# Low-part products last, ranks in two pieces, and a deeper split-ahead in a one-core decoder step

## The chip, the core and the metric

The kernel runs on one core of one Trainium2 chip. The metric is the device time of one execution in microseconds (us); several executions are made and their median is quoted. PE is the matrix engine (PEld its weight loads), DVE, ACT and POOL are the vector, scalar and GpSimd engines, SP issues most of the transfers.

## The reference

One layer of a decoder: 512 prompt tokens and 32 sample tokens of width 1024, through a mixer (projection, pooling, a stabilised mLSTM, an output projection) and then product-key retrieval over 16384 single-neuron experts:

```python
q = (xb @ w_q).reshape(blk, PEER_HEADS, 2, HALF_KEY)
s = jnp.einsum('nhpc,hpkc->nhpk', q, keys)
sv, si = lax.top_k(s, TOPK)                       # 16 of 128 keys, for each half
comb = sv[:, :, 0, :, None] + sv[:, :, 1, None, :]
top, sel = lax.top_k(comb, TOPK)                  # 16 of 256 pairs
eidx = ...                                        # the experts that the pairs name
g = jax.nn.softmax(top, axis=-1)
act = jax.nn.gelu(jnp.einsum('nd,nhkd->nhk', xb, u_tab[eidx]))
y = jnp.einsum('nhk,nhkd->nd', g * act, v_tab[eidx])
```

## The kernel before

**Products in two parts.** Every large float32 product is made of three matmuls: each operand is split into a high and a low part, and hi x hi, hi x lo and lo x hi are summed in PSUM (the accumulator banks). For weights ACT makes the high part `whi` (a rounding copy, line 443) and DVE or POOL the low part `wlo` = raw - whi (line 445). A weight block goes through three places: a load into one of four `raw` buffers (SP, line 418), the split into one of four `whi`/`wlo` pairs, and the products. The class `Weights` walks a list of blocks: `deep` is how many split blocks it holds ahead of the one in use, `early` how many loaded ones beyond that. The list also says which engine makes the low part.

**Where the three products stand.** `part` (called by `proj`, for the first projections and for the queries `half_q`), `out_mm` (the output projection), `uphase` (the experts' first table) and `ymm` (the second table) each issue hi·hi, hi·lo, lo·hi for every chunk before they go to the next one, so the low part of the weights is wanted by the third matmul.

**The retrieval.** 384 of the 512 prompt tokens are done densely: `uphase(b)` multiplies them by a block of 128 experts of `u_tab` (24 matmuls of 384 columns into `pH`, then a Gelu on ACT); there are 128 blocks, U0 to U127 below. `ymm` multiplies the gated activations by the block of `v_tab` (18 matmuls of 512 columns into six banks `Y`). The other 128 prompt tokens and the sample tokens gather their experts' rows one by one (POOL issues the gathers, DVE does the arithmetic).

**The order around the change.** The queries run in two halves (`halves`); four U blocks (`PRE`) are put among the second. DVE sorts the scores (`top16`, `best`). Then comes one loop, which mixes U blocks on PE with a generator `topks` on DVE: `ranks` (indices of the pairs), `topk` for five groups of tokens, transposes on PE (`gates_in`) and 48 groups of gate products (`gates_of`: one-hot tiles `E` and `P` on DVE, 16 matmuls each into `pg` on PE, a copy to `stage` on ACT, a write to DRAM `Gd`). Which comes next in the program is decided by a small model in that loop: `pe` and `dve` are its clocks, `PEU`, `PEG`, `LOU`, `GRP` its prices, `TOFF` DVE's lead time at the start, and each `yield` of `topks` a price in us. `lo_at` holds when low parts are ready. The loop may run blocks only up to `AHEAD - RES`; the rest up to `AHEAD` follow it and cover the time until the first gates are back from DRAM.

After the loop SP is given five loads of spilled activations (`ar`), the first load of gates (`load_g`, tile `gr`), more U blocks and the first blocks of `v_tab` (tile `vr`, which shares the four `raw` buffers). Activations of U blocks below `SPILL = AHEAD - RING` went to DRAM. In the last stage each V block (`vprep`, then `ymm`) is done alone until 13 activations are left on the chip, and from there with one U block each; `pace` spreads 320 gather steps over it.

The engines work their instructions in the order of the program, each its own; SP's transfers too are issued in order.

## Time and profile before

| | |
|---|---|
| three timed runs | 1651.47, 1658.17, 1670.41 us (median 1658.17) |
| the profiled execution | 1654.74 us, span 1653.0 us |
| PE busy / DVE busy / ACT busy / POOL busy | 94% / 82% / 38% / 42% of the span |
| mean granted clock of PE | 0.972 of full speed |
| transfers | 454.16 MB, mean 275 GB/s |

A timeline row gives the start, the duration, the engine, the source line, the operation, out<-in with shapes, how many, and in brackets how long the engine had been idle before and what ended that. A row of stretches gives start:end, length, and busy time of PE, PEld, DVE, ACT and POOL with their instructions, then the granted clock of PE (1.00 is 2.4 GHz; 0.5 would be 1.2 GHz all through), the busy share of the transfer engines and GB/s.

### The profile page before, as it was taken

Reading aid. Unit: us, or ns where it says so; the run is one execution under the profiler, and the core shown is the slowest. Engines: PE = TensorE matmul, PEld = TensorE weight load, DVE = VectorE, ACT = ScalarE, POOL = GpSimd, SP = SyncE. Lnnn points to the kernel's source line nnn. Section 1 sums busy time; section 2 is a strip of 40 time slices with the busy share of each in tenths; the row PEclk is TensorE's granted clock in tenths of the full one; section 3 lists DMA queues with packets and bytes.
Section 4 is the critical chain, followed back from the end, with each engine's and each line's share of the span. In section 5 each row is a group of like instructions: output and inputs, shape, how many; then the busy total and the mean of one; then the engine's idle time right before and its main releaser. Section 6 shows DMA issues by size and latency. Waiting matters only on the chain.

```text
span 1653.0 us, 25192 instructions
## 1 busy us (share of the span) xinstructions
PE 1560.3 (94%) x9293; PEld 1385.3 (84%) x9293; DVE 1349.8 (82%) x2738; ACT 630.5 (38%) x999; POOL 702.0 (42%) x517
## 2 busy tenths in 40 slices
PE   5999999897998999999999999999999999999994
PEld 3888777586998989998778899999999999999873
DVE  6644467698999899985888888988888898988986
ACT  4322223545533345553333333333333333333343
POOL 2343333456551000004233356656566666566615
PEclk9999988998999999999999999999999999999997
DMA  8544446554343558869999999999999999999981
GB/s 343 178 144 160 144 147 173 191 182 128 114 142 118 170 175 289 302 245 378 379 356 382 344 336 368 370 365 359 370 376 358 359 371 363 366 370 359 368 282 67
DMA packets 180272, 454.16 MB, mean 275 GB/s; under 512 B 23152, under 2 KB 83440, under 8 KB 178484
## 3 DMA queue, kind: packets, MB, share of 16 engines
q1 hardware_dynamic: 119448, 246.31, 43.5%
q0 software_dynamic: 46080, 167.79, 27.0%
q10 hardware_dynamic: 14620, 38.44, 6.2%
q8 instruction: 73, 1.20, 0.3%
q14 instruction: 51, 0.42, 0.1%
HBM read 412.34 MB, written 40.14 MB: 274 GB/s over the span
## 4 chain that ended last, share of the span: by engine, by line
PE 74%; DVE 13%; DMA 5%; issue 3%; ACT 2%; POOL 2%; SPq 0%; ACTq 0%; POOLq 0%; DVEq 0%
PE Y L160 27%; PE pH L160 27%; PE bk L160 10%; PE tb L160 4%; PE pg L160 3%; DMA gr<-Gd 2%; PE pm L160 1%; DVE wlo L445 1%; DMA wm<-in_w_mod_r_dram 1%; POOL wlo L445 1%; DMA raw<-in_u_b_dram 1%; PE tb L164 1%; DVE i L1108 1%; DVE scr L1106 1%; DVE scr L1111 1%
## 5 line engine op out<-in xcount | busy, mean ns | idle before, releaser
L1433 POOL DMA_INDIRECT rbuf<-in_u_tab_dram,eid x160 | 211.9, 1324 | 421.8 <-DMA ar<-Ad 235.3
L160 PE MATMUL pH<-u2hi,wlo 128*128 128x384 f32 x992 | 334.8, 338 | 6.9 <-DVE wlo L445 6.8
L160 PE MATMUL pH<-u2hi,whi 128*128 128x384 f32 x992 | 339.8, 343 | 0.4 <-ACT act L1192 0.4
L160 PE MATMUL pH<-u2lo,whi 128*128 128x384 f32 x992 | 335.1, 338 | 0.0
L1433 POOL DMA_INDIRECT rbuf<-in_v_tab_dram,eid x160 | 244.5, 1528 | 188.7 <-DVE y L1458 133.2
L160 PE MATMUL Y<-whi,chi 128*128 128x512 f32 x768 | 300.5, 391 | 5.3 <-ACT chi L1499 5.3
L160 PE MATMUL Y<-whi,clo 128*128 128x512 f32 x768 | 301.9, 393 | 3.5 <-DVE clo L1500 2.3
L160 PE MATMUL Y<-wlo,chi 128*128 128x512 f32 x768 | 301.3, 392 | 0.0
L443 ACT ACTIVATE whi<-raw 128x1024 fp32r<-128x1024 f32 (+1 forms) x193 | 203.0, 1055 | 218.7 <-issue 174.3
L443 ACT ACTIVATE whi<-vr 128x1024 fp32r<-128x1024 f32 x128 | 135.6, 1060 | 283.3 <-PE Y L160 243.2
L445 DVE TENSOR_TENSOR wlo<-vr,whi 128x1024 fp32r<-128x1024 f32 x128 | 156.7, 1224 | 91.7 <-ACT whi L443 87.9
L445 POOL TENSOR_TENSOR wlo<-raw,whi 128x1024 fp32r<-128x1024 f32 (+2 forms) x64 | 149.7, 2348 | 156.7 <-ACT whi L443 155.3
L1458 DVE SCALAR_TENSOR_TENSOR y<-rbuf,cf,y 128x1024 f32<-128x1024 f32 x158 | 202.5, 1282 | 0.9
L160 PEld LDWEIGHTS pH<-u2hi,wlo 128*128 128x128 f32 x992 | 186.9, 188 | 8.9 <-DVE wlo L445 8.9
L445 DVE TENSOR_TENSOR wlo<-raw,whi 128x1024 fp32r<-128x1024 f32 (+1 forms) x133 | 161.9, 1220 | 37.4 <-ACT whi L443 37.2
L160 PEld LDWEIGHTS pH<-u2hi,whi 128*128 128x128 f32 x992 | 187.2, 189 | 3.8 <-ACT act L1192 0.7
L160 PEld LDWEIGHTS pH<-u2lo,whi 128*128 128x128 f32 x992 | 187.1, 189 | 2.9
L160 PEld LDWEIGHTS Y<-whi,chi 128*128 128x128 f32 x768 | 144.8, 189 | 37.5 <-ACT chi L1499 7.3
L160 PEld LDWEIGHTS Y<-whi,clo 128*128 128x128 f32 x768 | 144.8, 188 | 34.3 <-DVE clo L1500 4.1
L160 PEld LDWEIGHTS Y<-wlo,chi 128*128 128x128 f32 x768 | 144.7, 188 | 30.1
L1446 DVE SCALAR_TENSOR_TENSOR rbuf<-rbuf,utok 128x1024 f32<-128x1024 f32 x128 | 156.1, 1222 | 0.0
L1192 ACT ACTIVATE act<-pH 128x384 f32<-128x384 f32 x124 | 59.4, 479 | 111.1 <-PE pH L160 111.1
(402 smaller groups left out, 2583.1 us busy)
## 6 DMA issues: line engine op xcount, KB each, us to landing
raw<-in_u_b_dram SPq DMA_DIRECT2D x128, 512.0 KB
vr<-in_v_tab_dram SPq DMA_DIRECT2D x128, 512.0 KB
wm<-in_w_mod_r_dram SPq DMA_DIRECT2D x48, 512.0 KB
gr<-Gd SPq DMA_DIRECT2D x32, 768.0 KB
Gd<-stage ACTq DMA_DIRECT2D x9, 2048.0 KB
raw<-in_w_q_b_dram SPq DMA_DIRECT2D x32, 512.0 KB
raw<-in_w_in_b_dram SPq DMA_DIRECT2D x20, 512.0 KB
Ad<-act ACTq DMA_DIRECT2D x40, 192.0 KB
```

The source lines that it names most:

```text
L160: nc.tensor.matmul(out, l, r, start=start, stop=stop, skip_group_check=True)
L164: nc.tensor.transpose(out, x, idn)
L443: nc.scalar.activation(hi, raw, AF.Copy)
L445: e.tensor_tensor(lo[:, d], raw[:, d], f32(hi[:, d]), op=ALU.subtract)
L1106: nc.vector.max(v[:, k], x)
L1108: nc.vector.max_index(i[:, k], v[:, k], x)
L1111: nc.vector.match_replace(x, v[:, k], x, -3.0e38)
L1192: nc.scalar.activation(x, p[:, 0:ND], AF.Gelu)
L1433: nc.gpsimd.indirect_dma_start(out=g, out_offset=None, in_=tab, in_offset=bass.IndirectOffsetOnAxis(ap=eid[t][:, k:k + 1], axis=0))
L1446: nc.vector.scalar_tensor_tensor(g, g, 1.0, u, op0=ALU.mult, op1=ALU.mult, accum_out=dots[:, k:k + 1])
L1458: nc.vector.scalar_tensor_tensor(y2[t], g, cf[:, k:k + 1], y2[t], op0=ALU.mult, op1=ALU.add)
```

## The change

Five things are changed.

1. In `part`, `out_mm`, `uphase` and `ymm` all products with the low part of the weights stand behind those with the high part: for a U block 16 matmuls with `whi`, then 8 with `wlo`; for `ymm` the two column halves alternate within each of the three products.
2. `ranks` becomes a generator with two prices (3.0 and 5.5) in place of one of 8.5, so U blocks' work may be put between its two pieces.
3. `WI.deep` is 3 in the loop (it was 2), and 2 again after it. The low part of one more U block is made on POOL (`PLO` = 4 in place of 3).
4. The loop's model: `TOFF` 14 in place of 10, low parts wanted `LOL` = 2.5 us after a block's start, `lo_at` with four places.
5. `AHEAD` 55 and `RES` 6 in place of 53 and 4. The loop may still run up to block 48; `SPILL` goes from 40 to 42.

```diff
-AHEAD = 53
+AHEAD = 55
-RES = 4
+RES = 6
+LOL = 2.50
+PLO = 4
-TOFF = 10.00
+TOFF = 14.00
...
     def part(p, w, m, i, dh, dl, cs=CORD):
         hi, lo = w[:2]
-        for c in cs:
-            for k, (x, u) in enumerate(((hi, dh), (hi, dl), (lo, dh))):
-                mm(p[:m, 0:WIDTH[i]], x[:, c, :], u[:, c, HALVES[i]],
-                   c == CORD[0] and k == 0, c == CORD[-1] and k == 2)
+        todo = [(c, x, u) for c in cs for x, u in ((hi, dh), (hi, dl))] + [(c, lo, dh) for c in cs]
+        for n, (c, x, u) in enumerate(todo):
+            mm(p[:m, 0:WIDTH[i]], x[:, c, :], u[:, c, HALVES[i]],
+               c == CORD[0] and n == 0, c == CORD[-1] and n == len(todo) - 1)
...
-    jobs += [(a["u_b"][b], 128, ON_POOL if b < ub + 3 else ON_DVE) for b in range(ub, NB)]
+    jobs += [(a["u_b"][b], 128, ON_POOL if b < ub + PLO else ON_DVE) for b in range(ub, NB)]
...
     def out_mm(p, t, c, w, n):
-        for i in range(2):
-            for k, (y, v) in enumerate(((yhi, hi), (ylo, hi), (yhi, lo))):
-                mm(p[i], y[:, c, cols_of[t]], v[:, 512 * i:512 * (i + 1)], n == 0 and k == 0, n == 7 and k == 2)
+        for ys in (((yhi, hi), (ylo, hi)), ((yhi, lo),)):
+            for i in range(2):
+                for y, v in ys:
+                    mm(p[i], y[:, c, cols_of[t]], v[:, 512 * i:512 * (i + 1)],
+                       n == 0 and y is yhi and v is hi, n == 7 and v is lo)
...
     def uphase(b, where=hbank):
-        for c in range(8):
-            for w, u in ((hi, u2hi), (hi, u2lo), (lo, u2hi)):
-                mm(p[:, 0:ND], w[:, c, :], u[:, c, DOFF:DOFF + ND], n == 0, n == 23)
-                n += 1
+        todo = [(c, hi, u) for c in range(8) for u in (u2hi, u2lo)] + [(c, lo, u2hi) for c in range(8)]
+        for n, (c, w, u) in enumerate(todo):
+            mm(p[:, 0:ND], w[:, c, :], u[:, c, DOFF:DOFF + ND], n == 0, n == 23)
...
         nc.vector.tensor_copy(cf_, ci)
+        yield 3.0
         ii = grl.tile([128, 16, HS], F16, name="ii")
...
         sx = grl.tile([128, HS], F32, name="sx2")
+        yield 5.5
         return ex, sx, ii, jj
...
-        r = ranks()
-        yield 8.5
+        r = yield from ranks()
...
+    WI.deep = 3
-    pe, dve, wait, freed, lo_at = 0.0, TOFF, [], [], [0.0, 0.0]
+    pe, dve, wait, freed, lo_at = 0.0, TOFF, [], [], [0.0] * PLO
...
-            pe = max(pe, lo_at.pop(0)) + PEU
-            dve = max(dve, pe - 2 * PEU) + LOU
-            lo_at.append(dve + 0.2)
+            pe = max(pe, lo_at.pop(0) - LOL) + PEU
+            if b + WI.deep > ub + PLO:
+                dve = max(dve, pe - PEU) + LOU
+                lo_at.append(dve + 0.2)
...
+    WI.deep = 2
...
     def ymm(b, t, parts=(slice(0, 512), slice(512, D))):
-        for d in parts:
-            y = Y[t][d.start // 512][:, d.start % 512:d.start % 512 + d.stop - d.start]
-            mm(y, ch[:, s], hi[:, d], b == 0, False)
-            mm(y, cl[:, s], hi[:, d], False, False)
-            mm(y, ch[:, s], lo[:, d], False, b == NB - 1)
+        for k, (c, v) in enumerate(((ch, hi), (cl, hi), (ch, lo))):
+            for d in parts:
+                y = Y[t][d.start // 512][:, d.start % 512:d.start % 512 + d.stop - d.start]
+                mm(y, c[:, s], v[:, d], b == 0 and k == 0, b == NB - 1 and k == 2)
```

What the loop's model makes of it, counted in PE's order of the two programs: before, 8 U blocks (U4 to U11) stand ahead of the first transposes, after, 11 (U4 to U14); 3, 4 and 4 blocks follow between the next transposes and the first gate products in both. The first gate products thus stand behind U22 before and behind U25 after. Then one U block and two groups of gate products alternate; in both programs six U blocks stand between the last gate products and the first V block, U47 to U52 before and U49 to U54 after, and after, the last three groups stand together with no U block among them. 40 V blocks are done alone before, 42 after.

On DVE, at the start of the loop, the low parts of U blocks (`wlo`) and `ranks` (`ex` to `jj`) stood before as

```order
L445 TENSOR_TENSOR wlo<-raw,whi 128x1024
L1239 TENSOR_TENSOR ex<-top 128x544
L1242 TENSOR_SCALAR rtmp<-sel 128x544
L1243 CAST rtmp<-rtmp 128x544
L1244 TENSOR_SCALAR rtmp<-sel 128x544
L1245 CAST rtmp<-rtmp 128x544
L1248 SCALAR_TENSOR_TENSOR rtmp<-rtmp 128x544
L1249 TENSOR_SCALAR rtmp<-rtmp 128x544
L1250 TENSOR_TENSOR ii<-rtmp 128x544
L1251 TENSOR_TENSOR rtmp<-rtmp 128x544
L1252 TENSOR_SCALAR rtmp<-rtmp 128x544
L1253 TENSOR_TENSOR jj<-rtmp 128x544
```

and stand now, on the same engine at the same place, as

```order
L447 TENSOR_TENSOR wlo<-raw,whi 128x1024 x2
L1241 TENSOR_TENSOR ex<-top 128x544
L1244 TENSOR_SCALAR rtmp<-sel 128x544
L1245 CAST rtmp<-rtmp 128x544
L1246 TENSOR_SCALAR rtmp<-sel 128x544
L1247 CAST rtmp<-rtmp 128x544
L447 TENSOR_TENSOR wlo<-raw,whi 128x1024
L1251 SCALAR_TENSOR_TENSOR rtmp<-rtmp 128x544
L1252 TENSOR_SCALAR rtmp<-rtmp 128x544
L1253 TENSOR_TENSOR ii<-rtmp 128x544
L1254 TENSOR_TENSOR rtmp<-rtmp 128x544
L1255 TENSOR_SCALAR rtmp<-rtmp 128x544
```

Before, one `wlo` (U7's) stands ahead of `ranks` and the next behind it; now U8's and U9's stand ahead of it and U10's between its pieces, while U7's has gone to POOL. Ahead of the first `P` DVE makes 17 low parts before and 20 after.

On SP, at the end of the loop, the loads of U blocks (`raw`), spilled activations (`ar`), the first gates (`gr`) and the first V blocks (`vr`) stood before as

```order
L418 DMA raw<-in_u_b_dram 128x1024 x47
L1485 DMA ar<-Ad 128x384 x5
L418 DMA raw<-in_u_b_dram 128x1024
L1471 DMA gr<-Gd 128x12x128
L418 DMA raw<-in_u_b_dram 128x1024 x3
L1477 DMA vr<-in_v_tab_dram 128x1024 x4
```

and stand now, on the same queue, as

```order
L420 DMA raw<-in_u_b_dram 128x1024 x50
L1491 DMA ar<-Ad 128x384 x5
L1477 DMA gr<-Gd 128x12x128
L420 DMA raw<-in_u_b_dram 128x1024 x3
L1483 DMA vr<-in_v_tab_dram 128x1024 x4
```

Before, U51's load stands between the activations and the gates; now no U load does, and U53's, the last one ahead of the activations, stands in the run of 50.

## Rows read from the trace of the kernel before

**Rows 1.** The page, busy time of each engine (share of the span) and instructions.

```profile
PE 1560.3 (94%) x9293; PEld 1385.3 (84%) x9293; DVE 1349.8 (82%) x2738; ACT 630.5 (38%) x999; POOL 702.0 (42%) x517
```

**Rows 2.** Stretches: the loop's first part, its gate products, and the last stage.

```profile
514.00:605.00 91.00, 81.65 (x477) 79.62 (x476) 85.17 (x148) 33.85 (x45) 0.00 (x0) 0.96 0.46 148
605.00:735.00 130.00, 130.00 (x1187) 126.70 (x1186) 125.07 (x151) 74.79 (x127) 0.00 (x0) 1.00 0.77 282
...
900.00:1100.00 200.00, 200.00 (x984) 178.70 (x983) 174.52 (x224) 70.94 (x99) 106.86 (x75) 1.00 0.99 355
```

**Rows 3.** What PE waited for: total us, times, longest.

```profile
PE bk L160 <- POOL wlo L445: 7.5, 4, 3.3
PE pH L160 <- DVE wlo L445: 6.8, 5, 3.4
```

**Rows 4.** Timeline of PE, output projection and end of the first query half.

```profile
313.58 0.80 PE L160 MATMUL tb<-wlo,yhi 128*128 128x512 f32 x1 [0.63 <-POOL wlo L445]
...
413.56 3.40 PE L160 MATMUL tb<-con,ut 128*32 128x128 f32 x64 [3.54 <-POOL ut L1016]
```

**Rows 5.** Timeline of PE, the loop up to the first gate products.

```profile
516.87 0.45 PE L160 MATMUL pH<-u2hi,wlo 128*128 128x384 f32 x1 [2.64 <-DVE wlo L445]
524.77 0.45 PE L160 MATMUL pH<-u2hi,wlo 128*128 128x384 f32 x1 [3.42 <-DVE wlo L445]
594.52 1.87 PE L160 MATMUL pg<-P,E 128*128 128x128 f16 x16 [2.70 <-DVE P L1356]
```

**Rows 6.** Stretches of 5 us, PE alone: busy, clock, transfer share, GB/s.

```profile
525.00:530.00 5.00, 5.00 (x21) 0.66 0.62 209
...
770.00:775.00 5.00, 2.58 (x6) 0.66 1.02 401
```

**Rows 7.** The chain that ended last: a U block and a V block in the last stage.

```profile
942.64 4.21 PE pH L160 x24
946.85 4.12 PE Y L160 x18
```

**Rows 8.** Timeline of DVE in the loop.

```profile
540.99 1.23 DVE L445 TENSOR_TENSOR wlo<-raw,whi 128x1024 fp32r<-128x1024 f32 x1 [1.48 <-ACT whi L443]
...
571.63 1.23 DVE L445 TENSOR_TENSOR wlo<-raw,whi 128x1024 fp32r<-128x1024 f32 x1 [2.33 <-ACT whi L443]
...
593.18 1.29 DVE L1356 TENSOR_TENSOR P<-E,gp 128x1024 f16<-128x1024 f16 x2
```

**Rows 9.** Timeline of ACT in the loop: Gelu of U4, the split behind it, Gelu of U5.

```profile
505.48 0.49 ACT L1192 ACTIVATE act<-pH 128x384 f32<-128x384 f32 x1 [2.87 <-PE pH L160]
...
506.43 1.06 ACT L443 ACTIVATE whi<-raw 128x1024 fp32r<-128x1024 f32 x1 [0.46 <-ACT act L1192]
509.70 0.49 ACT L1192 ACTIVATE act<-pH 128x384 f32<-128x384 f32 x1 [2.20 <-PE pH L160]
```

**Rows 10.** Timeline of PE, ACT and SP at the first V block.

```profile
771.30 0.59 PE L160 MATMUL Y<-whi,chi 128*128 128x512 f32 x1 [1.92 <-ACT chi L1499]
773.00 0.79 PE L160 MATMUL Y<-whi,clo 128*128 128x512 f32 x1 [1.11 <-POOL clo L1500]
...
769.78 1.06 ACT L443 ACTIVATE whi<-vr 128x1024 fp32r<-128x1024 f32 x1 [5.76 <-DMA vr<-in_v_tab_dram]
...
744.31 0.38 SPq L418 DMA_DIRECT2D raw<-in_u_b_dram  x1
...
761.02 13.37 SPq L1477 DMA_DIRECT2D vr<-in_v_tab_dram  x4
```

**Rows 11.** A stretch of 15 us among the V blocks done alone.

```profile
880.00:895.00 15.00, 15.00 (x68) 12.43 (x67) 13.16 (x20) 6.05 (x8) 6.28 (x5) 1.00 1.06 384
```

**Rows 12.** Timeline of PE in one V block: one bank, then the next.

```profile
899.86 0.39 PE L160 MATMUL Y<-whi,clo 128*128 128x512 f32 x1
900.09 0.39 PE L160 MATMUL Y<-wlo,chi 128*128 128x512 f32 x1
900.31 0.39 PE L160 MATMUL Y<-whi,chi 128*128 128x512 f32 x1
```

More of the change, by code (lines that the diff above doesn't have):

```diff
@@ L1185, in uphase @@
         p = where()
-        n = 0
-        for c in range(8):
-            for w, u in ((hi, u2hi), (hi, u2lo), (lo, u2hi)):
-                mm(p[:, 0:ND], w[:, c, :], u[:, c, DOFF:DOFF + ND], n == 0, n == 23)
-                n += 1
+        todo = [(c, hi, u) for c in range(8) for u in (u2hi, u2lo)] + [(c, lo, u2hi) for c in range(8)]
+        for n, (c, w, u) in enumerate(todo):
+            mm(p[:, 0:ND], w[:, c, :], u[:, c, DOFF:DOFF + ND], n == 0, n == 23)
         x = actp.tile([128, ND], F32, name="act", tag="act", bufs=RING)
```

## The prediction

> **What bounds the kernel now.** I read the busy time of the engines, then the stretches, then what PE waited for, and last the timeline around each long wait. PE is busy 94% of the span [rows 1]; in the gate products and the last stage it has no idle time at all, while DVE has 4% and 13% [rows 2]. So the bound is PE's own work, and an edit that moves matmuls without removing any can win only what PE loses elsewhere: idle time, and time at a lower granted clock behind it. A U block costs 4.21 us and a V block 4.12 us [rows 7], the same in either order of the products. PE's waits for low parts are 7.5 us (queries, by POOL) and 6.8 us (U blocks, by DVE) [rows 3]; the change aims at these. The timeline shows where they matter.
>
> **The U blocks at the start of the loop.** PE stops 2.64 us at 516.87 and 3.42 us at 524.77, each time for a `wlo` that DVE makes behind its sorting and behind `ranks` [rows 5]; after the second stop the granted clock of the next 5 us is 0.66 [rows 6], so 3.4 of them were at 1.2 GHz: 1.7 us of work lost. Now U7's low part is made on POOL, U8's and U9's ahead of `ranks` and U10's inside it; moreover a block now asks for its low part after 16 matmuls, not after 2, which is 14 × 4.21/24 = 2.46 us later. U7 can start when U6 ends (about 513.9, from the Gelu rows [rows 9]: U4 505.48, U5 509.70, so one block in 4.22), and wants its low part at 516.7; U8 wants its own at 520.9, and DVE has it at about 517. Both waits go, with the clock's fall: 2.64 + 3.42 + 1.7 = 7.8 us.
>
> That is not yet the gain, because the next meeting of PE and DVE is at the first gate products, where PE waited 2.70 us for `P` until 594.52 [rows 5]. Here DVE decides, so I follow DVE. Its last `P` pair is put out at 593.18, 1.29 us long [rows 8]. Ahead of that DVE now makes 20 low parts, not 17: 3 × 1.2 = 3.6 us more. It also waits for `whi`, because ACT makes the split of block k+4 (k+3 before) only behind the Gelu of block k, whose end frees the buffer; from the Gelu's start to the end of that split are 506.43 + 1.06 − 505.48 = 2.0 us [rows 9]. Before, such waits were 1.48 and 2.33 [rows 8], reached by DVE at 539.5 and 569.3. After, the same places stand behind three more low parts: 543.1 and, with the first wait 0.9 longer, 573.8. The splits wanted there are U17's, behind the Gelu of U13 (505.48 + 9 × 4.22 + 2.0 = 545.5), and U24's, behind that of U20 (505.48 + 16 × 4.22 + 2.0 = 575.0, and I add 0.6 for two sets of transposes, my estimate). The waits are 2.4 and 1.8, 4.2 in place of 3.8. So `P` is 3.6 + 0.4 = 4.0 us later: PE starts the gate products at 598.5. It would be free at about 595, so it still waits 3 to 4 us there, with the same fall of the clock as now, costed at nothing on both sides. But by then it has done three more U blocks, 3 × 4.21 = 12.6 us. **Gain: 12.6 − 4.0 = 8.6 us.** If DVE waits for no split, `P` is there at 594.3 and PE, free only at 595, decides: 12.1. If its waits double, it is 8.6 − 4.2 = 4.4.
>
> The gate products then run as before: PE has no idle time there, DVE 4.9 us of 130 [rows 2]. One block fewer stands in them, so two blocks in all have moved out of the last stage. They are no loss, since PE is the bound in both places, and no gain either.
>
> **Into the first V block.** Six U blocks cover the way of the gates in both programs, so the gates come at the same distance. PE waited 1.92 for `chi` and 1.11 for `clo` [rows 10]; the clock was 0.66 in those 5 us [rows 6]. `chi` stands on ACT behind the split of the first `vr`, which waited for its load until 769.78 [rows 10]. That load was issued at 761.02, behind three U loads, and U51's load, issued at 744.31 [rows 10] ahead of the gates, shared the queue. Now U53's load is out long before, so the queue holds 512 KB less ahead of `vr`: at the 401 GB/s moved there [rows 6] that is 1.3 us, and at most the whole wait with its lower clock, 3.0 + 1.7 = 4.7, or nothing if the write of the gates sets the time. I take 1.5, near the lower end, because this is time of transfers and not of order. `clo` is wanted one matmul later, 4.12/18 = 0.23 us.
>
> **Low parts last elsewhere.** In the output projection the last wait on POOL, 0.63 us at 313.58 [rows 4], shrinks by two matmuls of 0.23: 0.5 us, between 0 and 0.6. In the first query half the waits [rows 3] shrink by up to 14 of 24 matmuls, at most 7.5 us in all, but I cost them at nothing: this half ends with PE waiting 3.54 us at 413.56 for POOL's `ut` [rows 4], the end of a chain of DVE, ACT and POOL work on the layer norm, and PE comes to that wait however early. If that cover were gone, up to 4 us would count.
>
> **More activations spilled.** Two blocks more are written and read, 4 × 192 KB; two U loads of 512 KB leave the last stage. On PE nothing; in transfers the last stage gets 0.66 MB less.
>
> **Sum.** 8.6 + 1.5 + 0.5 = 10.6 us; of this I give back 0.8 for later gate loads that PE, being earlier, meets sooner (my estimate, half of the 1.5): 9.8. Against the profiled execution, 1654.7 us (span 1653.0 and 1.7 around it), that is 1644.9. The median of the runs shown, 1658.2, stands 3.4 above that execution and the fastest 3.3 below, so I forecast **1645 us**.
>
> **A rule against it.** The last stage moves 355 GB/s with the transfer engines busy 0.99 [rows 2], and PE is never idle: which of the two paces it? In the V blocks done alone 384 GB/s were held over 15 us [rows 11], so the stage has some 8% left. The Trainium skill, DMA: Bandwidth & Descriptors (section Specifications), gives about 358 GB/s as the limit of HBM for one core; by that the last stage would be at its limit, and two U blocks taken out of it would save transfers, not PE's time. The trace disagrees: 384 is above it.
>
> **Rivals.**
> *The last stage is paced by transfers.* For: busy share 0.99, and two blocks at 4.21 leave PE's side, but only 0.66 MB the transfers'. Then the stage shortens by 0.66 MB at 355 GB/s, 1.9 us, instead of 8.4; 6.5 us are given back: 1651. Against: PE's zero idle time and the 384 GB/s. The skill's limit named above would make the same time. Chance 0.14.
> *DVE is later still at the first gate products.* The splits wait for PE, and PE for `P`: with the doubled waits the stage gains 4.4 and the sum is 5.6: 1649. For: DVE has only 5.8 us free of 91 there [rows 2]. Chance 0.12.
> *More than I count.* DVE waits for no split and the first V block opens without a wait: 12.1 + 4.7 + 0.5 = 17.3, 1637. Chance 0.13.
> *Slower: turning between two banks costs PE time.* `ymm` went to the other bank behind every third matmul and now goes behind every one: 4 × 3 = 12 more turns a block, 1536 in all. It takes 9.8/1536 = 6.4 ns a turn to eat the gain, and 17 ns to be 1% slower: at 20 ns, 30.7 us, the time is 1676. Against: in the rows a product behind a turn starts 0.22 us after the one before, without a turn 0.23 [rows 12], so the cost is not seen. Chance 0.05.
> *No change that is seen*, because the loop's end is set elsewhere: 1655, 0.04.
>
> **How the numbers follow.** My case, 1640 to 1650, has 0.52. The range that holds 8 in 10 takes in the rivals at 1649 and 1651 and most of the case at 1637: **1637 to 1657**, the upper end 2 us above the profiled execution for the runs' own spread. About 1% is what a measurement of this kernel can tell from no change. Faster by over 1% (below 1641.6 against the median, 1638.2 against the profiled execution) are the case of more and the lower edge of mine: 0.15. Slower by over 1%: 0.05 and a little: 0.06. Within 1%: 0.79.
>
> **What would show it.** Right: no wait of PE for `wlo` between 510 and 530, and no fall of the clock there; the first gate products at 598 ± 2 behind 22 U blocks, with PE waiting 2 to 4 us; the first V block at the same time as before or up to 3 us earlier; in the last stage PE without idle time, at a few GB/s more. Wrong: if PE waits for `wlo` later among U11 to U25, or if the first `vr` is again the last to come; if idle time of PE in the last stage grows by the 6 us that the loop has won, transfers pace it; if a V block takes more than 4.12 us, turning between banks costs.

## The result and the profile after

The changed kernel took 1645.82 us (median of 18 runs), the kernel before 1659.26 us in the runs beside them (median of 18). The ratio is 0.9908, with a 95% interval from 0.9889 to 0.9927: a gain of 0.92%, 12 to 18 us. One of the 18 runs took 2541.03 us at a granted clock of 0.558; the ratio leaves it out, and without it the median is 1645.72. The median forecast was 1645.0 us, so the time was met. The gain was not: against the same kernel's median it is 13 to 15 us, where my sum gave 9.8. The sum stood on a profiled execution that lay 4.5 us below its kernel's median, and that difference made up for the part I missed: that the time came out within 1 us is luck. As the rest shows, the parts of the sum were further off than their total.

The profiled execution of the changed kernel took 1639.83 us, its span is 1638.0 us (before: 1654.74 and 1653.0). The page, busy time of each engine:

```profile
PE 1548.3 (95%) x9293; PEld 1378.1 (84%) x9293; DVE 1349.4 (82%) x2737; ACT 639.6 (39%) x999; POOL 698.2 (43%) x518
```

The stretches that answer to [rows 2], [rows 6] and [rows 11] (busy time of PE, PEld, DVE, ACT and POOL, granted clock, transfer share, GB/s):

```profile
514.00:605.00 91.00, 87.34 (x525) 86.85 (x524) 85.73 (x135) 37.07 (x49) 0.00 (x0) 0.98 0.55 171
605.00:735.00 130.00, 130.00 (x1188) 126.62 (x1187) 124.94 (x151) 74.75 (x127) 0.00 (x0) 1.00 0.75 276
900.00:1100.00 200.00, 198.76 (x973) 176.56 (x972) 172.95 (x223) 73.72 (x99) 105.97 (x75) 1.00 0.99 359
525.00:530.00 5.00, 5.00 (x31) 5.00 (x30) 4.83 (x10) 4.04 (x5) 0.00 (x0) 1.00 0.75 235
770.00:775.00 5.00, 5.00 (x13) 3.83 (x13) 5.00 (x9) 1.70 (x4) 4.38 (x3) 0.50 0.85 301
880.00:895.00 15.00, 15.00 (x67) 12.20 (x66) 12.37 (x18) 6.16 (x8) 5.93 (x5) 1.00 1.05 384
```

PE gained 5.7 us of busy time in the first stretch, and the fall of the clock at 525 is gone (1.00, where it was 0.66). At 770 the clock is at its lower level all through (0.50), as part of that stretch was before (0.66).

What PE waited for (total us, times, longest), and its timeline at the places the prediction named:

```profile
PE bk L162 <- POOL wlo L447: 4.4, 3, 2.1
PE pg L162 <- DVE P L1360: 3.7, 1, 3.7
```

```profile
594.33 1.50 PE L162 MATMUL pg<-P,E 128*128 128x128 f16 x16 [3.65 <-DVE P L1360]
...
760.21 0.44 PE L162 MATMUL pH<-u2hi,whi 128*128 128x384 f32 x1 [0.77 <-ACT act L1194]
...
767.90 0.73 PE L162 MATMUL Y<-whi,chi 128*128 128x512 f32 x2 [3.22 <-ACT chi L1505]
...
769.60 1.22 PE L162 MATMUL Y<-whi,clo 128*128 128x512 f32 x2 [0.96 <-POOL clo L1506]
```

Against [rows 3] the waits for DVE's `wlo` in the loop are gone and those for POOL's are shorter. Against [rows 5] the wait for `P` is longer (3.65 for 2.70), and against [rows 10] the wait for `chi` is longer too (3.22 for 1.92).

To compare executions I take four marks of PE: the end of the first query half (the start of the 64 small matmuls at 413.56 in [rows 4]; the second half and four U blocks stand between it and the loop), the first gate products, the first V block, and the end of the span. All numbers are us from profiled executions, differences of marks rounded to 0.1; the programs are those of the experiments below.

| kernel | end of first query half | to first gate products | to first V block | to the end |
|---|---|---|---|---|
| before | 413.6 | 180.9 | 176.8 | 881.7 |
| after | 408.0 | 186.3 | 173.6 | 870.1 |
| e_pre | 414.8 | 181.7 | 178.3 | 883.2 |
| e_uymm | 412.2 | 177.8 | 177.9 | 876.4 |
| e_sched | 411.3 | 186.3 | 175.8 | 873.1 |
| e_order | 408.0 | 180.3 | 177.0 | 880.8 |
| e_vmix | 414.4 | 190.7 | 174.3 | 868.9 |
| e_gpre0 | 416.7 | 191.0 | 169.0 | 868.6 |
| e_toff18 | 414.7 | 190.2 | 177.4 | 865.2 |
| e_plo8t22 | 414.4 | 190.1 | 178.2 | 868.2 |
| e_pool4 | 401.7 | 185.8 | 175.4 | 869.6 |
| e_pool2 | 401.3 | 186.3 | 175.6 | 868.3 |
| e_pool4g0 | 401.3 | 186.1 | 169.2 | 869.2 |
| e_gr2 | 401.1 | 185.1 | 170.2 | 868.9 |

Between the first two rows of the table: −5.6 ahead of the query half's end, −7.2 to the first gate products (5.4 later, with three U blocks, 12.6 us, more done), +1.0 to the first V block (one U block fewer stands there: 3.2 earlier, less 4.2), and −3.2 in the last stage (11.6 earlier, less two U blocks). The sum is −15.0, the difference of the two spans.

### The profile page after: what moved, and what is told of

Read it like the earlier page. It is cut to its first block, busy times and chain, and to the rows that moved or that the text cites. A ratio compares the mean times of both kernels' runs of the same rounds, so it can differ in the third digit from the quotient of the medians.

```text
span 1638.0 us, 25202 instructions
## 1 busy us (share of the span) xinstructions
PE 1548.3 (95%) x9293; PEld 1378.1 (84%) x9293; DVE 1349.4 (82%) x2737; ACT 639.6 (39%) x999; POOL 698.2 (43%) x518
## 4 chain that ended last, share of the span: by engine, by line
PE 72%; DVE 14%; DMA 7%; ACT 3%; issue 2%; POOL 1%; SPq 0%; ACTq 0%; DVEq 0%; POOLq 0%
PE pH L162 29%; PE Y L162 24%; PE bk L162 10%; PE tb L162 4%; DMA gr<-Gd 3%; PE pg L162 3%; DVE wlo L447 2%; PE pm L162 1%; DMA vr<-in_v_tab_dram 1%; DMA wm<-in_w_mod_r_dram 1%; PE tb L166 1%; DMA rbuf<-in_u_tab_dram,eid 1%; DVE ost L251 1%; ACT whi L445 1%; DVE x L987 1%
## 5 line engine op out<-in xcount | busy, mean ns | idle before, releaser
L1439 POOL DMA_INDIRECT rbuf<-in_v_tab_dram,eid x160 | 237.0, 1481 | 178.2 <-DVE y L1464 125.5
L162 PE MATMUL Y<-whi,chi 128*128 128x512 f32 x768 | 240.7, 392 | 5.4 <-ACT chi L1505 5.4
L162 PE MATMUL Y<-whi,clo 128*128 128x512 f32 x768 | 241.0, 393 | 2.3 <-DVE clo L1506 1.2
L162 PE MATMUL Y<-wlo,chi 128*128 128x512 f32 x768 | 239.4, 390 | 0.0
L162 PE MATMUL pH<-u2hi,wlo 128*128 128x384 f32 x992 | 194.4, 337 | 0.0
L162 PEld LDWEIGHTS pH<-u2hi,wlo 128*128 128x128 f32 x992 | 175.8, 188 | 0.0
```

The costliest lines, as they stand in the source:

```text
L162: nc.tensor.matmul(out, l, r, start=start, stop=stop, skip_group_check=True)
L1439: nc.gpsimd.indirect_dma_start(out=g, out_offset=None, in_=tab, in_offset=bass.IndirectOffsetOnAxis(ap=eid[t][:, k:k + 1], axis=0))
```

## The experiments

**Which part is worth what.** Four kernels that each hold a part of the change.

*e_order*: the kernel before with the low parts last in `part`, `out_mm`, `uphase` and `ymm`; nothing else.

```diff
-        for c in range(8):
-            for w, u in ((hi, u2hi), (hi, u2lo), (lo, u2hi)):
+        todo = [(c, hi, u) for c in range(8) for u in (u2hi, u2lo)] + [(c, lo, u2hi) for c in range(8)]
+        for n, (c, w, u) in enumerate(todo):
...
```

> The kernel before with the low parts last in all four functions; nothing of the schedule is changed. My theory, from the two traces: the order is worth the 5.6 us by which the changed kernel reached the loop earlier (the matmuls at 413.56 before, 407.97 after), and in the loop nothing, since DVE puts out the first P when it did: PE's waits for wlo at 516.87 and 524.77 (2.64 and 3.42 us) shrink by up to 2.46 each and come back as a longer wait for P (2.70 before, about 6 now). So the end of the first query half at 408, first gate products at 594.5 - 5.6 = 589, a span of 1653.0 - 5.6 = 1647.4, a ratio of 0.9966. Rival 1: the 5.6 us are spread between two executions and not the order: the loop is entered at 413.5, ratio 1.000. Rival 2: the order also saves time in the loop and the last stage: ratio 0.994 or below.

Measured: 0.9964 (0.9947 to 0.9981). The query half ended at 408.0 and the first gate products stood at 588.3, as expected. The way there was not: of the waits for `wlo` one shrank from 2.64 to 0.23 us and the other stayed (3.41), and the wait for `P` was 3.64, not about 6.

*e_sched*: the changed kernel with the old order of products in all four functions.

> The changed kernel with the old order of products (low part third) in all four functions; the schedule alone is changed. My theory: up to the loop it runs as before (the matmuls at 413.56 at the same time within 0.5 us); in the loop the three more U blocks ahead of the first gate products are worth 12.6 us less the 5.4 by which P came later in the changed kernel, 7.2, and the waits for wlo stay gone because the low parts are made earlier; the last stage keeps its 3.2. Span 1653.0 - 10.4 = 1642.6, ratio 0.9937. Rival 1: without the 2.46 us of later demand PE waits for wlo again at U7 to U10 (some 2 to 4 us with a fall of the clock) but P is what decides, so the time is the same and only the wait for P is shorter. Rival 2: those waits do cost: span 1646 to 1650, ratio 0.996 to 0.998. If the 5.6 us ahead of the loop appear here too, they are not the order's.

Measured: 0.9944 (0.9920 to 0.9967). The way to the first gate products is 186.3, as in the changed kernel, so in that execution the later demand for low parts added nothing to the schedule there, and no wait for `wlo` came back. The product of the two ratios, 0.9964 × 0.9944, is 0.9908, that of the whole change: schedule and order are worth about 9 and 6 us, and within the intervals they add.

*e_pre* has the new order only in `part` and `out_mm`, *e_uymm* only in `uphase` and `ymm`.

> The kernel before with the low parts last only in part and out_mm, the products ahead of the loop. My theory: this alone gives the 5.6 us ahead of the loop (the matmuls at 413.56 come at 408) by shorter waits of PE for POOL's low parts, and nothing behind it: span 1647.4, ratio 0.9966. Prediction on record: 0.5 us, ratio 0.9997, because the waits saved come back as a wait for the chain of DVE, ACT and POOL at the layer norm. Rival: spread, the loop is entered anywhere between 408 and 414 in each of these runs whatever the order.

Measured: 0.9994 (0.9966 to 1.0021), the query half's end at 414.8. My theory, formed on the two traces, that the order brings the 5.6 us ahead of that mark, falls by the marks (below); its ratio is the edge of the interval. So e_order met its ratio for a wrong reason. The 0.5 us of the prediction lie within the interval.

> The kernel before with the low parts last only in uphase and ymm. My theory: up to the loop as before (413.5), PE's waits for wlo in the loop shrink from 6.8 us to under 2 and the fall of the clock at 525 goes, but the first P comes when it did (593.2) and PE waits the more for it; V blocks take 4.12 us as before: span 1653.0, ratio 1.000. Rival 1: the clock's fall that is gone counts: 1.7 us, ratio 0.999. Rival 2: turning between two banks behind every product costs time in the 128 V blocks: ratio above 1.002 and V blocks longer than 4.12.

Measured: 0.9944 (0.9922 to 0.9967). Here my theory (no gain) fell: the first `P` did not come when it did before. Counted from the Gelu of U4, the first gate products came at 89.0 us before, 87.0 in e_order and 85.3 in e_uymm, with DVE's program the same in all three. e_order holds all of this and more and gained less; the intervals overlap, and I read no difference into it. In the trace the way to the first gate products is 3.1 us shorter than before and the last stage 5.3 shorter; rival 2, a cost of turning between banks, is out: V blocks are shorter, not longer.

The 5.6 us ahead of the query half's end are spread between executions. Three kernels with before's program up to there have the mark at 411.3, 412.2 and 413.6 (mean 412.4); seven with the new order at 408.0, 408.0, 414.4, 414.4, 414.7, 414.8 and 416.7 (mean 413.0). Stretches of the same program at the same place, first of the kernel before, then of e_sched, show where that comes from:

```profile
200.00:225.00 25.00, 23.53 (x168) 17.09 (x167) 17.27 (x58) 6.99 (x20) 6.05 (x9) 0.80 0.48 142
250.00:275.00 25.00, 22.35 (x101) 18.86 (x102) 22.25 (x42) 7.06 (x10) 12.16 (x17) 0.81 0.49 119
```

```profile
200.00:225.00 25.00, 23.30 (x188) 18.22 (x188) 18.93 (x62) 8.50 (x21) 6.58 (x10) 1.00 0.56 167
250.00:275.00 25.00, 22.36 (x100) 18.00 (x98) 21.14 (x40) 6.72 (x10) 11.05 (x15) 0.86 0.51 129
```

PE is busy as long in both, but the granted clock over 200 to 225 is 0.80 in one and 1.00 in the other: in both PE waited 1.47 us at 216 to 217, and at that wait the clock fell in one execution and not in the other.

**V blocks: turning between banks, or the weights?** A V block takes 4.09 us after and 4.12 before, a U block 4.22 and 4.21. The chain in the last stage, first of the kernel before, then of after:

```profile
1030.18 4.12 PE Y L160 x18
1034.30 4.21 PE pH L160 x24
```

```profile
1031.35 4.22 PE pH L162 x24
1035.57 4.09 PE Y L162 x18
```

*e_vmix*, a single run (1650.12 us), takes four orders of `ymm`'s six products in turn, by b mod 4.

```diff
-        for k, (c, v) in enumerate(((ch, hi), (cl, hi), (ch, lo))):
-            for d in parts:
+        order = ([(k, d) for d in (0, 1) for k in (0, 1, 2)], [(k, d) for k in (0, 1, 2) for d in (0, 1)],
+                 [(0, 0), (1, 1), (2, 0), (0, 1), (1, 0), (2, 1)], [(0, 0), (2, 0), (1, 0), (1, 1), (0, 1), (2, 1)])[b % 4]
...
```

> The changed kernel with four orders of a V block's six products per token group, block by block in turn (b mod 4). The weights of a matmul are chi or clo; the six products go to two banks. 0: the order of before (weights ch cl ch / ch cl ch, one turn of bank within the six). 1: the order of after (ch ch / cl cl / ch ch, a turn behind every matmul, the same weights twice in a row). 2: the weights in the order of before, with a turn behind every matmul. 3: one bank at a time, with the same weights twice in a row (ch ch cl / cl ch ch). In the traces block 0's order takes 4.12 us and block 1's 4.09 in the last stage. Theory A, turning between banks is what is faster: order 2 takes 4.09 and order 3 takes 4.12 (it turns as often as order 0). Theory B, the same weights twice in a row are what is faster: order 2 takes 4.12, order 3 takes 4.09 (three repeats, as order 1). On record I had the opposite sign as a rival: a turn costs time (4.12 to over 4.2). The span is not what this run is for: about 1640 + 1.5.

Measured, from the starts of 71 V blocks: 4.09 us in all four orders. Both theories fall. The span of about 1641.5 was missed too (1648.3), ahead of the V blocks, as the section on DVE and POOL shows. What the shorter blocks share is the U block ahead of them: e_order, e_uymm, after and e_vmix have the new `uphase` and 4.09, before, e_pre and e_sched the old one and 4.12. In the V blocks done alone the rate of matmuls is the same with either order (353 in 80 us in e_sched, 354 in after). So 0.026 us a pair of U and V block (0.031 less in the V block, 0.005 more in the U block, means over more than 70 of each) comes with the order in the U block; for 73 pairs 1.9 us. Why is not settled.

**The first V block.** *e_gpre0*: ten gathers that POOL issued ahead of the first V block are put behind it.

```diff
-GPRE = 2
+GPRE = 0
```

> The changed kernel with GPRE 0 in place of 2: the ten gathers that POOL issued before the first V block now stand behind it. Theory: the first vr, which was issued at 753.13 and came at 766.38, shared the queue with six gathers of 512 KB issued from 752.85 on; at 400 GB/s these are 7.9 us, so without them vr comes some 5 to 8 us earlier, PE's waits of 0.77, 3.22 and 0.96 at 760 to 770 go, and so does the time at a clock of 0.63 behind them (9 us, 3 of them lost): the first V block opens at about 764, and the last stage begins 5 to 7 us earlier. DVE's first steps on gathered rows then wait for gathers issued behind clo, which costs nothing if the low parts of two V blocks ahead are made: span 1632 to 1634, ratio 0.987. Rival 1: vr is held by something else (the gates' write and load, 768 KB, and three U loads): it comes at 764 or later and the ratio is that of the changed kernel, 0.991. Rival 2: the later gathers cost DVE and the queue in the V blocks what was won: first V block earlier, the last stage longer, ratio 0.991 or above.

Timelines of SP (`gr`, `vr`), POOL and ACT in the changed kernel:

```profile
744.03 0.37 SPq L1477 DMA_DIRECT2D gr<-Gd  x1
...
753.13 17.86 SPq L1483 DMA_DIRECT2D vr<-in_v_tab_dram  x4
```

```profile
752.85 1.53 POOL L1439 DMA_INDIRECT rbuf<-in_u_tab_dram,eid  x1 [9.23 <-DMA Gd<-stage]
...
766.38 1.06 ACT L445 ACTIVATE whi<-vr 128x1024 fp32r<-128x1024 f32 x1 [6.22 <-DMA vr<-in_v_tab_dram]
```

and of e_gpre0:

```profile
762.82 12.14 SPq L1483 DMA_DIRECT2D vr<-in_v_tab_dram  x4
...
770.32 1.06 ACT L445 ACTIVATE whi<-vr 128x1024 fp32r<-128x1024 f32 x1 [1.32 <-DMA vr<-in_v_tab_dram]
...
798.87 1.22 PE L162 MATMUL Y<-whi,chi 128*128 128x512 f32 x2 [5.65 <-ACT chi L1505]
```

With the gathers in the queue the first `vr` needs 13.25 us from issue to use, without them 7.5. PE does not wait at the first V block, and the way there is 169.0 us against 174.3 in e_vmix, the same program in all else up to there, on the same chip: 5.3 us. The theory stands for that place. Part is given back behind it: PE waits 5.65 us for `chi` at 798.87. The span expected, 1632 to 1634, was not reached (1645.3): this execution, like e_vmix, lost time ahead of the first gate products. The ratio, 0.9887 (0.9856 to 0.9918), is not to be told from the changed kernel's.

**More U blocks, or more of them on POOL.**

```diff
-TOFF = 14.00
+TOFF = 18.00
```

> The changed kernel with TOFF 18 in place of 14: 24 U blocks ahead of the first gate products in place of 22, and so two fewer between the groups of gate products. Theory: as by the step on record, each block ahead is worth 4.2 us of PE time and puts P off by 1.2 to 1.8 us, until PE is no longer the one that waits: the wait of 3.65 us goes, P comes 2.4 to 3.6 us later, PE gets there later than P, and the loop gains 3.65 us and the lower clock behind it, 4 to 5 us in all: ratio 0.988. Rival: the loop is then bound by DVE at its gate products (DVE was busy 125 of 130 us there), the two blocks taken out of there leave PE waiting for P at its end by 3 to 5 us, and the ratio stays at 0.991 or is above it.

Measured: 0.9929 (0.9901 to 0.9957), the rival. The first half of the theory holds: two more U blocks are done ahead of the first gate products in the same time (190.2 against 190.7 in e_vmix). But the way from there to the first V block has two fewer (8.4 us) and is 3.1 longer, 11.5 lost. PE does not wait for the first `P`, but 2.40 us for a later one at 608.36. PE's timeline behind that:

```profile
741.08 1.09 PE L162 MATMUL pg<-P,E 128*128 128x128 f16 x16 [0.92 <-DVE P L1360]
...
743.42 2.29 PE L162 MATMUL pg<-P,E 128*128 128x128 f16 x32 [1.25 <-DVE P L1360]
...
776.03 0.69 PE L162 MATMUL pH<-u2hi,whi 128*128 128x384 f32 x1 [9.25 <-ACT act L1194]
```

The waits for `P` that I expected are 2.2 us. The large one I did not: 9.25 us at a U block, for ACT, which itself waited for the block's load:

```profile
774.55 1.06 ACT L445 ACTIVATE whi<-raw 128x1024 fp32r<-128x1024 f32 x1 [15.64 <-DMA raw<-in_u_b_dram]
```

I read this as the gathers, the gates and the U loads meeting as in the changed kernel, with less work of PE to cover them; no run tests it.

*e_plo8t22*: PLO 8 and TOFF 22.

> The changed kernel with the low parts of eight U blocks on POOL (PLO 8, four before) and TOFF 22: 23 U blocks stand ahead of the first gate products, 22 before. Theory A, POOL's idle time in the loop is free: DVE makes three low parts fewer ahead of P (four go to POOL, one block is added), so P comes 3.6 us earlier and PE, which has one block more to do, does not wait for it (3.65 before); the time at a lower clock behind that wait goes as well: 4 to 5 us, span 1633.5, ratio 0.988. Theory B, from the trace: a DVE sum of two tiles that meets a POOL low part ends only when that one ends (128x32 scr: 0.17 us alone, up to 1.6 beside POOL; the one at 502.19 ends with POOL's at 503.4), so each low part on POOL holds DVE by 1 to 2 us: four of them take back 4 to 8 us, P comes no earlier or later than in the changed kernel, and the ratio is 0.990 to 0.993.

Measured: 0.9944 (0.9919 to 0.9969); the interval overlaps that of the changed kernel, and no gain is seen. One U block more is done ahead of the first gate products in 190.1 us (4.8 better than e_vmix), and 8.1 are lost behind them, with a wait of 9.06 us at 776.61 like the one above. The wait for `P` is 3.93 us. So this run does not decide between its theories, and the next paragraph shows why neither could: the wait for `P` follows something else.

**What `P` follows.** PE's wait for `P` is 3.62 to 3.65 us in ten of the fourteen executions, though DVE came to its first low part of the loop anywhere from 102.6 to 110.3 us behind the mark. In the changed kernel, the Gelu of U20, the split behind it (U24's) and the low part that DVE makes of that split:

```profile
569.35 0.49 ACT L1194 ACTIVATE act<-pH 128x384 f32<-128x384 f32 x1 [2.19 <-PE pH L162]
...
570.30 1.06 ACT L445 ACTIVATE whi<-raw 128x1024 fp32r<-128x1024 f32 x1 [0.46 <-ACT act L1194]
```

```profile
571.40 1.22 DVE L447 TENSOR_TENSOR wlo<-raw,whi 128x1024 fp32r<-128x1024 f32 x1 [1.79 <-ACT whi L445]
```

From here DVE does not wait again, and the first gate products start 22.93 us later. Before, they start 22.89 us behind the same kind of row (571.63 in [rows 8]), and in thirteen of the fourteen executions the distance from DVE's last wait for a split is 22.9. Only in e_toff18 is it 36, and there PE does not wait at the first gate products. So PE waits at the gate products for a chain that its own U20 set going. A DVE that comes earlier waits longer for the splits (the first of the two waits is 1.59 us in e_pool4, 1.49 in after, 0.39 in e_vmix), and `P` stays where it is. Counted from the Gelu of U4, the first gate products come at 92.9 us in all five executions of the changed kernel's loop in which PE does not wait for `wlo` (after and the four with pieces below), and at 98.8 in the two in which it does (e_vmix, e_gpre0). A late DVE costs time there, through that wait and the clock behind it.

**DVE waits for POOL.** Two executions of one program up to the V blocks, after and e_vmix, differ by 4.4 us between the query half and the first gate products, and e_vmix has the wait that the change was to remove:

```profile
525.77 1.59 PE L162 MATMUL pH<-u2hi,wlo 128*128 128x384 f32 x5 [4.09 <-DVE wlo L447]
```

DVE was busy nearly all that time in both (2.7 and 2.3 us of waits). Its sums of 128x32 in `best` (line 1120) take 0.17 us alone. Beside POOL's low parts, in e_vmix:

```profile
473.57 1.54 DVE L1120 TENSOR_TENSOR scr<-scr 128x32 f32<-128x32 f32 x1
```

```profile
472.67 2.39 POOL L447 TENSOR_TENSOR wlo<-raw,whi 128x1024 fp32r<-128x1024 f32 x1 [1.82 <-ACT whi L445]
```

473.57 + 1.54 = 475.11, and 472.67 + 2.39 = 475.06: DVE's small sum ends when POOL's instruction ends. Between the mark at the query half and DVE's first low part of the loop there are 6 such sums of over 1 us before, 8 after, 10 in e_vmix and in e_gpre0, of 13 each (the expectation below says 11 of 15; an eleventh that was held there is a sum of 128x16); the three sums of `best` take 14.2, 16.4, 22.5 and 22.6 us in all, and DVE has that first low part 102.0, 104.6, 110.1 and 110.3 us behind the mark. The Trainium skill, SBUF — State Buffer (section Who interferes with whom), says that a DVE instruction with two inputs in SBUF contends with a GpSimd instruction that reads SBUF, over a shared read interface, and calls the shared ports an exclusive lock. The trace agrees, with these ends; the rule speaks against the step that put U7's low part on POOL, and I had not weighed it. What that step cost can be read: U7's low part, the last that POOL makes, held one sum in after (1.23 us in place of 0.17). The other sums are held by low parts that POOL made before the change too.

*e_pool4* makes each low part on POOL in four instructions, *e_pool2* in two.

```diff
-    ON_POOL, ON_DVE = ((nc.gpsimd, slice(None)),), ((nc.vector, slice(None)),)
+    ON_POOL, ON_DVE = ((nc.gpsimd, slice(0, 2)), (nc.gpsimd, slice(2, 4)), (nc.gpsimd, slice(4, 6)), (nc.gpsimd, slice(6, 8))), ((nc.vector, slice(None)),)
```

> The changed kernel with each low part on POOL made in four pieces of 128x256 (in the queries and the first U blocks) in place of one instruction of 128x1024 (2.40 us). What it is for: in two profiled executions of the same program up to the V blocks (the changed kernel, and the one with four V orders) DVE's sorts between 410 and 520 end 104.6 and 110.1 us behind the end of the first query half, because 8 and 11 of DVE's 15 sums of 128x32 (0.17 us alone) took 1.1 to 2.1 us, each ending when POOL's low part ended; in the later one PE waits 4.09 us for wlo at 525.77. Theory A: DVE waits for POOL's instruction, so with pieces of about 0.85 us no such sum takes over 0.9 us; DVE has its first low part of the loop at 99 to 102 us behind the end of the half in every execution, PE does not wait for wlo, P comes 3 to 8 us earlier and PE's wait of 3.65 for it goes: 4 to 9 us below the changed kernel's median, ratio 0.986. Rival B: those sums wait for something else (PE, a semaphore): they stay at 1.1 to 2.1 us, ratio 0.991. Rival C: the pieces make POOL's low part longer than 2.46 us late (four times about 0.35 us more), PE waits for POOL in the queries by more than is won: ratio 0.993 or above.

> As the kernel before it, with two pieces of 128x512 (about 1.3 us each). Theory A: DVE's sums beside POOL take at most 1.3 us, about half of the wait remains, the low part is only some 0.3 us later: DVE's first low part 101 to 105 us behind the end of the half, ratio 0.988. Rival B as there: no change in the sums, ratio 0.991. Rival D: DVE does not get between two pieces that follow at once, the sums wait for the second piece too: as with one instruction.

Measured: 0.9865 (0.9830 to 0.9900) and 0.9866 (0.9825 to 0.9906). The sums in e_pool4:

```profile
470.40 0.41 DVE L1120 TENSOR_TENSOR scr<-scr 128x32 f32<-128x32 f32 x1
470.73 0.85 DVE L1121 TENSOR_TENSOR scr<-scr 128x112 f32<-128x112 f32 x1
471.51 0.69 DVE L1124 TENSOR_TENSOR scr<-scr 128x16 f32<-128x16 f32 x1
```

```profile
469.33 2.84 POOL L447 TENSOR_TENSOR wlo<-raw,whi 128x256 fp32r<-128x256 f32 x4 [0.16 <-ACT whi L445]
```

No sum takes more than 0.9 us, which is theory A against rival B: it is POOL's instruction that they wait for. But now each of the three waits for a piece of its own, so the three take 16.0 us in all (16.7 in e_pool2), and DVE has its first low part 104.0 us behind the mark (104.8 in e_pool2). I had expected 99 to 102; what I missed is that the second and third sum, which ran behind POOL's end before, now meet the next piece. The wait for `P` is 3.65 us still, as it must be if `P` follows U20. So the pieces make DVE hardly earlier than in the profiled execution of after (104.6); all three profiled executions with pieces and the fourth below are as that one (185.1 to 186.3 to the first gate products) and none has the wait for `wlo`. That theory A's ratio, 0.986, was met is therefore luck. The other gain, not foreseen, is ahead of the mark: it stands at 401.1 to 401.7 in all four, against 408.0 to 416.7. One part of it shows in PE's waits in e_pool4:

```profile
PE bk L162 <- POOL wlo L447: 0.6, 2, 0.4
```

3.8 us less than after. The rest is not taken apart, and the intervals of e_pool4 and e_pool2 still touch that of the changed kernel.

*e_pool4g0*: four pieces and GPRE 0.

> Four pieces on POOL, and GPRE 0 (the ten gathers behind the first V block). If both theories hold the gains add, since one is ahead of the first gate products and the other at the first V block, and PE bounds both: GPRE 0 took 5 us out of the way from the first gate products to the first V block (174.3 to 169.0), the pieces 4 to 9 ahead of it: ratio 0.982 to 0.984, 1630 to 1633 us. If the loop is bound by DVE further on, the earlier start comes back as waits for P, and the ratio is that of GPRE 0 alone, 0.989.

Measured: 0.9842 (0.9808 to 0.9876); 169.2 us to the first V block as in e_gpre0, 401.3 and 186.1 as in e_pool4. The edits add. As in e_gpre0, PE waits at the fifth V block, there too behind DVE, which waits for the second load of gates (8.86 us, until 777.32):

```profile
778.55 1.22 PE L162 MATMUL Y<-whi,chi 128*128 128x512 f32 x2 [5.49 <-ACT chi L1505]
```

*e_gr2*: the loads of gates two V blocks earlier besides.

```diff
-        if b % 4 == 0 and b:
-            load_g(b)
+        if b % 4 == 2 and b + 2 < NB:
+            load_g(b + 2)
```

> Four pieces on POOL and GPRE 0, and every load of gates issued two V blocks earlier (the second one right behind the third vr, ahead of the ten gathers). In the kernel with the two edits alone PE waited 5.5 us for chi at 778.55: the second gr was issued at 758.45, behind the gathers that POOL issued from 753.4 on, and came at 777.3. Theory: what GPRE 0 gave at the first V block was half given back there, by the same queue; with the load ahead of the gathers it comes by 760 and the wait goes, with the lower clock behind it: 5 to 7 us, ratio 0.979 to 0.981. Rival: 768 KB more ahead of the fourth vr make that one late (up to 2 us of wait in the third or fourth V block), or the gathers that DVE steps wait for come later still: ratio 0.983 to 0.985.

Measured: 0.9797 (0.9765 to 0.9829), 1628.22 us (median of 5). PE has no wait at the fifth V block any more, but one of the same length three blocks further. The timelines of PE, of SP and of ACT:

```profile
790.60 1.22 PE L162 MATMUL Y<-whi,chi 128*128 128x512 f32 x2 [5.51 <-ACT chi L1505]
```

```profile
767.05 0.43 SPq L1477 DMA_DIRECT2D gr<-Gd  x1
767.53 11.38 SPq L1491 DMA_DIRECT2D ar<-Ad  x1
779.02 1.23 SPq L1483 DMA_DIRECT2D vr<-in_v_tab_dram  x1
...
```

```profile
789.08 1.06 ACT L445 ACTIVATE whi<-vr 128x1024 fp32r<-128x1024 f32 x1 [10.68 <-DMA vr<-in_v_tab_dram]
```

The gates are not late now; the next `vr` is, because SP stood 11.4 us at a load of activations ahead of it. So the trace shows the wait put off, not removed, and the span of the profiled execution is only 0.5 us shorter (1625.3 for 1625.8). That the ratio is 0.45% lower than that of e_pool4g0 is not explained by it, and the intervals overlap. Both kernels beat the one before and the changed one: 0.9797 and 0.9842 lie outside the interval of 0.9908.

## Why the prediction was right or wrong

*What bounds the kernel.* Right: PE, and edits won what PE lost in idle time and at the lower clock. No run showed transfers pacing the last stage: with two U blocks fewer it became 11.6 us shorter, not 1.9, and 384 GB/s were held again at 880. The rival at 1651 is out, and the rule of the Trainium skill named with it (DMA: Bandwidth & Descriptors, Specifications, 358 GB/s) does not bind this kernel.

*The loop, 8.6 us: right in size, with one reason wrong.* In the profiled execution of after both waits for `wlo` and the clock's fall are gone, and PE waits 3.65 us for `P` (2 to 4 predicted). Counted from the end of the query half the gain is 7.2, because `P` is 5.4 us later and not 4.0. But the difference lies ahead of the loop. From that mark to the Gelu of U4 PE did 670 matmuls without idle time, before and after, at different granted clocks:

```profile
413.56:505.48 91.92, 91.92 (x670) 0.98 0.39 125
```

```profile
407.97:501.39 93.42, 93.42 (x670) 0.97 0.39 123
```

The work is the same, so the 1.5 us are the clock's. In e_vmix, which has the order of after, the stretch took 91.94 at 0.99, so they are spread and not the change's. From the Gelu of U4 on, `P` is 3.9 us later (92.94 for 89.04) with 12.6 us more work done: a gain of 8.7. The step "Here DVE decides" was the wrong one. DVE came to the loop 2.6 us later than before, which the sum did not have, and `P` did not show it, because the split of U24 decides. The number held because the prediction took the time of that split from PE's own blocks: 70.1 us behind the Gelu of U4, measured 70.0. A cost was put at nothing all the same: DVE's sums waiting for POOL. In e_vmix and e_gpre0, where ten of those of 128x32 were held, PE waited 4.09 us for `wlo` and the gain from the mark was 2.8 and 2.5; so the loop's gain differs from execution to execution. "DVE is later still" was a rival at 0.12 for another reason, waits for splits; those came to 1.49 and 1.79 us, less than the 4.2 I had summed.

*The first V block, 1.5 us: wrong.* The step that failed is "the queue holds 512 KB less ahead of `vr`", which I priced as transfers ahead of `vr` in SP's order. `vr` was issued 7.9 us earlier than before, but used only 3.4 earlier, and PE waited 1.3 longer for `chi`. Relative to PE's work the stretch lost 1.0 us. e_gpre0 shows what I left out: POOL's gathers, which wait for the same write of the gates and then share the transfers with U and V loads whatever SP's order. In the prediction POOL stands at that place only as the maker of `clo`.

*Ahead of the loop, 0.5 us: not contradicted by e_pre* (1.0 us, between −3.5 and 5.6), which is too wide to confirm it. The 5.6 us in the two profiles are spread, with the clock falling at the same wait in one execution and not in another. Reading them as the change's, as I did at first, would have been an error.

*The last stage, nothing: 3.2 us were gained.* The sum took a V block at 4.12 us whatever the order of the products; the order in the U blocks gave 1.9 through shorter V blocks; the rival that turning between banks costs time is out, and of the other sign none is left either, since all four orders in e_vmix took 4.09 us. The rest lies in short waits for `chi` and `clo` behind 780 us, 5.7 us in all before and 3.3 after, whose places shift from run to run; I can't split it further.

*More than I count, 0.13.* The time of 1637 was not reached by the median, and not by its mechanism: DVE still waited for splits, and the first V block still opened with a wait.

## What to carry to other kernels

An idle engine isn't a free one: before work is moved to GpSimd, look for DVE instructions with two inputs beside it, and see in the trace whether the short one ends when the long one ends; if so, try the long one in pieces, and count what several short ones in a row then wait. Before an engine is made faster because another waits for it, look for the last thing it waited for itself: here that was the waiting engine's own work of 25 us earlier, and the wait stayed at 3.65 us. A profiled execution is one draw: a gain in a stretch that the edit doesn't touch is first compared over executions of the same program (here 408 to 417 us at one mark). When a stall is put down to a late load, count every queue that fills at that moment, the gathers of another engine too, and look for the stall a few blocks further on when it has gone.

## What the runs showed of the hardware that I had not expected

A DVE sum of 0.17 us took up to 2.3 us beside a GpSimd instruction of 2.4 us and ended within 0.05 us of it; with GpSimd's work in pieces of 0.7 us, three sums in a row each waited for one piece. Once held, DVE came back into the next low part: its sums stood 8.4 us apart, twice the 4.2 us between POOL's low parts, where they stand 7.0 apart when free.

A V block of 18 matmuls is 0.031 us shorter behind a U block whose last eight matmuls take the low part, whatever its own order.

The granted clock over 25 us in the same part of the program was 0.80 in one execution and 1.00 in another, with PE busy for 23.5 and 23.3 us of them and the same wait of 1.47 us in both.
